# A transformer layer on one core: the seven products of w_o in another order, added up in PSUM banks

## The chip, the cores and the metric

The kernel runs on 1 core of a Trainium2 chip. A core has five engines with an instruction queue each: TensorE (PE, with PEld for its weight loads), VectorE (DVE), ScalarE (ACT), GpSimd (POOL) and SyncE (SP); 16 DMA engines move data between DRAM and the core's own memories, SBUF (128 partitions) and PSUM (here eight banks of 128 x 512 float32, into which TensorE writes). The metric is the time of one execution in microseconds; given is the median of three runs.

## The reference

One layer on x of 512 tokens by 2048 channels, in float32:

```python
h = rms_norm(x, pre_mix_g);  z = h @ w_in            # q, k, v (1024 each) and u (1024)
a = chunked_attention(q, k, v, rel_bias)              # 8 heads of 128
p = multiscale_pool(u, pool_w, pool_scale)            # windows 2, 4, 8, 16: mean of the window
                                                      # minus the token, times pool_w per group
m = concat([a, p]) @ w_o                              # (512 x 2048) @ (2048 x 2048)
x = x + rms_norm(m, post_mix_g)
h = rms_norm(x, pre_ffn_g)
up = causal_dwconv(h @ w_up)                          # 2 x 5632 columns
y = (gelu(up[:, :5632]) * up[:, 5632:]) @ w_down
x = x + rms_norm(y, post_ffn_g)
```

The change lies in the line of m and in the two below it.

## The kernel before, in words

**Products.** A float32 operand is split into a rounded part (hi, fp32r) and the rest (lo): `split` (L138) has ACT round (L140, or L143 with a scale) and DVE subtract (L141, L144). `mm3` (L161) multiplies with three matmuls: hi by hi, hi by lo, lo by hi (L162, L164, L165).

**Weights.** `Weights` goes through a list of slices (`specs`) in the order of use. A slice of 128 x 1024 is loaded by SP (L152) into one of five raw buffers, at most two slices ahead of its split, and split into one of four pairs of buffers, four slices ahead of the matmuls. So the split of a slice waits for its data and for TensorE's end with the slice four before it.

**w_o.** The mixing matrix `mixT` (attention and pooled channels, transposed) times w_o is cut into 2 x 2 blocks: tokens 0 to 255 and 256 to 511, input halves, output halves of 1024 columns. Instead of eight block products there are seven (numbers 1 to 7) of sums and differences of blocks. The left factors (a11, s3, a12, n1, s2, s4, a22) are made by DVE from `mixT` and split; the sums of w_o's blocks for products 5, 6, 7 and 4 were added up in DRAM earlier. `wo_product(i, cc, ...)` makes one product for one half cc of 512 columns: four weight slices of 24 matmuls into two banks. After a slice of every product but the first it takes one step of `ready_blocks`, which readies six parts of w_down's first blocks: an SP load (`rw`, L843), four steps later the split, then two stores, after which the buffer takes the next load.

The order before is 1, 7, 2, 5, 6, 3, 4. Each product gets new banks. ACT copies products 1, 7 and 5 out (`copy_out`), DVE adds the others to rows in SBUF (`add_out`); three adds of 128 x 2048 (L946, L948, L949) join the rows: `y12 += y16`, `y16 += y7`, `y7 += y12`. A block of rows is then squared and summed by ACT (`square`, L910), multiplied by the gain by DVE (`scaled`, L915), normed (`norm`, L963 to L968, one step on POOL) and added to the residual x (`x2`, L980). `turn_back` transposes it (L995, TensorE) for the next stage, and `split` scales the result into `gT`.

**The pooled channels.** The last window's differences come from `pool_keep(3, 1, u7)`: sums by DVE (L732) into `tmp` (L737 to L740), split into dh and dl. `pool_mix(3)` multiplies the two differences (0 and 1) with `pool_w` (slice pm3): twelve matmuls in two banks, which ACT writes into the last part of `mixT` (L756).

**The first gate products.** `gate_part` multiplies the first slices of w_up with `gT` of tokens 0 to 255; between the parts the transposes of tokens 256 to 511 and their gate parts follow.

**Order.** TensorE runs in the order in which the code is written. The other engines' order is made by the framework's scheduler when the program is built, and is fixed then; each engine runs its list from the top and stands still while the first instruction waits.

```python
ps1 = [wo_product(1, cc, a11) for cc in range(2)]
...
pool_mix(3, keep_mix)
```

Of the kernel before, what the change touches and what calls it, by code (L numbers as in the profile page):

```python
# [15 lines left out]
P = 128  # L16
# [65 lines left out]
def encoder_layer(ctx: ExitStack, tc: tile.TileContext, x, xT, vecs, rel, post_mix, post_ffn,  # L82
# [160 lines left out]
    WO = 1, 7, 2, 5, 6, 3, 4  # L243
    wo_sum = {i: [dram.tile([P, 8, 512], F32, name=f"wt{i}{cc}") for cc in range(2)] for i in (7, 5, 6, 4)}
# [28 lines left out]
    for i in WO:  # L273
        for cc in range(2):
            specs += wo_specs(i, cc)
        if i == 1:
            specs += pm_spec(3)
# [12 lines left out]
    def sums_in_dram():  # L290
# [27 lines left out]
        for step, i, at in ((copy, 7, (1, 1)), (add, 7, (0, 1)), (copy, 5, (0, 0)), (add, 5, (0, 1)),  # L318
                            (copy, 6, 5), (add, 6, (1, 1)), (copy, 4, 6), (add, 4, (1, 0))):
            yield from wo_step(step, i, at)  # L320
# [292 lines left out]
    with tc.tile_pool(name="p1", bufs=2, reuse_waits="tile") as p1:  # L613
# [241 lines left out]

        def wo_product(i, cc, left, between=None):
            ps = [bank(f"m{i}{cc}{t}") for t in range(2)]
            if cc and i in (2, 5, 6, 3):
                more_sums(1)
            for q in range(4):  # L860
                w = weights.get(f"wo{i}_{cc}_{q}")
                for j in range(2):
                    kb = 2 * q + j
                    for t in range(2):
                        mm3(ps[t], tuple(v[:, kb, t * P:(t + 1) * P] for v in left), part(w, j), kb == 0, kb == 7)
# [8 lines left out]
        ps1 = [wo_product(1, cc, a11) for cc in range(2)]  # L874

        for v, w in zip(half(0, 0), half(0, 1)):
            nc.vector.tensor_sub(v, v, w)
        s3 = wo_left("s3", 0, 0)
        pool_mix(3, keep_mix)

    x2d = [dram.tile([P, D], F32, name=f"x2d{t}") for t in range(2, NT)]

    with tc.tile_pool(name="p2", bufs=1, reuse_waits="tile") as p2:
# [4 lines left out]
        y16, y7 = rows2("y16"), rows2("y7")  # L888
# [15 lines left out]
        def add_out(y, cc, ps, other=None):  # L904
            for t in range(2):
                nc.vector.tensor_add(y[:, t, columns(cc)], ps[t], (other or y)[:, t, columns(cc)])
# [10 lines left out]
        for cc in range(2):  # L917
            copy_out(y16, cc, ps1[cc])
        a12 = wo_left("a12", 1, 0)
        for cc in range(2):  # L920
            copy_out(y7, cc, wo_product(7, cc, s3))

# [3 lines left out]
        y11 = rows2("y11")  # L926
        for cc in range(2):
            add_out(y11, cc, wo_product(2, cc, a12), y16)

        for v, w in zip(half(0, 0), half(1, 1)):  # L930
# [5 lines left out]
        y12 = rows2("y12")  # L936
        for cc in range(2):
            copy_out(y12, cc, wo_product(5, cc, n1))
# [4 lines left out]
        for cc in range(2):  # L943
            add_out(y16, cc, wo_product(6, cc, s2))

        nc.vector.tensor_add(y12, y12, y16)  # L946
        a22 = wo_left("a22", 1, 1, [acc8(f"a22{p}", "A", F32R).rearrange("p (a b) -> p a b", a=8) for p in "hl"])
        nc.vector.tensor_add(y16, y16, y7)  # L948
        nc.vector.tensor_add(y7, y7, y12)  # L949
        y21, y22 = y16, y7  # L950
        for t in range(2):
# [796 lines left out]
```

## Time and profile before

| what | us |
|---|---|
| median of 3 runs | 1858.12 |
| lowest and highest | 1855.53, 1862.51 |
| span of the profiled execution | 1857.4 |
| TensorE busy in it | 1843.6 |
| VectorE busy | 1540.8 |
| ScalarE busy | 1082.3 |
| products of w_o in it (first to last matmul) | 389.8 to 550.1 |
| first gate matmul | 551.9 |

The profile is of one execution, and its span is that execution's own time. A row of the timeline shows the start, the length, the engine, the line, the operation with its tiles (output, arrow, inputs), and in brackets how long the engine had stood idle and what released it. Buffer numbers are left out of names, so `wo_1r` is the second slice of four of some product, as loaded, `wo_1h` and `wo_1l` its two parts, and `m` a bank of a product. Matmuls are pipelined: the time between two starts is what one costs. The numbers in a row of a table by window are the stretch, its length, busy times of PE, PEld, DVE, ACT and POOL (with counts), the granted clock, and the DMA engines' share and GB/s.

### The profile page before, as it was taken

How to read it: one execution, taken by the hardware profiler on the slowest of the kernel's cores; microseconds unless marked ns; L12 is line 12 of the kernel's file. 1: busy time of each engine (PE TensorE's matmuls, PEld its weight loads, DVE VectorE, ACT ScalarE, POOL GpSimd, SP SyncE). 2: the span in 40 equal slices, each digit the busy share in tenths (PEclk: the TensorE clock that was granted, in tenths of full speed). 3: DMA queues.
4: the chain of work that ended last, by engine and by line, in shares of the span. 5: the costliest groups of instructions: out<-in, count | busy, mean ns of one | idle time of the engine just before them, and what ended most of it. 6: DMA issues, size and time to landing. Idle time of an engine off the chain costs nothing.

```text
span 1857.4 us, 25457 instructions
## 1 busy us (share of the span) xinstructions
PE 1843.6 (99%) x9598; PEld 1584.8 (85%) x9598; DVE 1540.8 (83%) x1804; ACT 1082.3 (58%) x1376; POOL 303.2 (16%) x402
## 2 busy tenths in 40 slices
PE   9999999999999999999999999999999999999998
PEld 7888888888878888888888888888888888888886
DVE  6988777887698988888888888888887899899876
ACT  7654455456464666566666665656655655565553
POOL 3411000100000122212222122121121001111101
PEclk9999999999999999999999999999999999999999
DMA  8599978999994798988888888899888967777785
GB/s 319 174 318 297 320 232 236 267 255 331 348 328 144 186 213 195 208 210 195 203 198 206 209 199 198 204 206 202 200 176 293 363 220 175 193 210 178 176 229 159
DMA packets 139338, 426.01 MB, mean 229 GB/s; under 512 B 11920, under 2 KB 15376, under 8 KB 133520
## 3 DMA queue, kind: packets, MB, share of 16 engines
q0 software_dynamic: 54864, 173.56, 46.1%
q1 hardware_dynamic: 84352, 250.84, 38.4%
q8 instruction: 75, 1.23, 0.3%
q14 instruction: 47, 0.39, 0.1%
HBM read 370.35 MB, written 104.33 MB: 256 GB/s over the span
## 4 chain that ended last, share of the span: by engine, by line
PE 93%; DMA 3%; DVE 2%; ACT 1%; issue 1%; SPq 0%; DVEq 0%; POOL 0%; POOLq 0%; ACTq 0%
PE qa L170 18%; PE qa L176 10%; PE qg L170 9%; PE qg L176 5%; PE qd L170 4%; PE pa L164 4%; PE pa L165 4%; PE pa L162 4%; PE qd L176 2%; PE pg L164 2%; PE pg L165 2%; PE pg L162 2%; PE m L164 2%; PE m L165 2%; PE m L162 2%; PE v L164 2%
## 5 line engine op out<-in xcount | busy, mean ns | idle before, releaser
L140 ACT ACTIVATE wfh<-wx 128x1024 fp32r<-128x1024 f32 x192 | 203.4, 1059 | 152.7 <-PE qg L170 55.4
L170 PE MATMUL qa<-gT,wfh 128*128 128x512 f32 x1152 | 288.6, 392 | 0.0
L141 DVE TENSOR_TENSOR wfl<-wx,wfh 128x1024 fp32r<-128x1024 f32 x192 | 234.7, 1222 | 59.8 <-ACT wfh L140 44.8
L170 PEld LDWEIGHTS qa<-gT,wfh 128*128 128x128 f32 x1152 | 207.2, 189 | 37.1
L1365 POOL DMA_DIRECT2D wx<-in_w_up x122 | 104.7, 858 | 502.2 <-DVE wfl L141 473.8
L140 ACT ACTIVATE wfh<-wy 128x1024 fp32r<-128x1024 f32 x96 | 101.7, 1060 | 109.3 <-PE qg L170 57.9
L170 PE MATMUL qg<-h,wfh 128*128 128x512 f32 x656 | 162.2, 389 | 0.9 <-ACT zb L1421 0.9
L176 PE MATMUL qa<-gT,wfl 128*128 128x256 f32 x1152 | 161.2, 283 | 0.1
L176 PEld LDWEIGHTS qa<-gT,wfl 128*128 128x128 f32 x1152 | 151.6, 191 | 4.3 <-ACT zm L1425 0.3
L170 PEld LDWEIGHTS qg<-h,wfh 128*128 128x128 f32 x656 | 122.9, 188 | 26.7 <-ACT zb L1421 1.3
L141 DVE TENSOR_TENSOR bl<-b,bh 128x2048 fp32r<-128x2048 f32 x56 | 127.2, 2287 | 19.1 <-ACT bh L140 11.7
L140 ACT ACTIVATE bh<-b 128x2048 fp32r<-128x2048 f32 x56 | 106.1, 1913 | 55.1 <-DVE b L1129 22.8
L141 DVE TENSOR_TENSOR wfl<-wy,wfh 128x1024 fp32r<-128x1024 f32 x96 | 117.2, 1221 | 10.9 <-ACT wfh L140 6.4
L162 PE MATMUL pa<-bh,ah 128*128 128x512 f32 x320 | 124.5, 389 | 0.0
L164 PE MATMUL pa<-bl,ah 128*128 128x512 f32 x320 | 124.5, 389 | 0.0
L165 PE MATMUL pa<-bh,al 128*128 128x512 f32 x320 | 124.5, 389 | 0.0
L141 DVE TENSOR_TENSOR wfl<-wz,wfh 128x1024 fp32r<-128x1024 f32 x48 | 58.7, 1224 | 54.1 <-PE qa L170 54.1
L176 PEld LDWEIGHTS qg<-h,wfl 128*128 128x128 f32 x656 | 89.5, 190 | 6.4
L170 PE MATMUL qd<-gT,wfh 128*128 128x512 f32 x384 | 94.9, 389 | 0.0
L176 PE MATMUL qg<-h,wfl 128*128 128x256 f32 x656 | 91.5, 282 | 0.0
L170 PEld LDWEIGHTS qd<-gT,wfh 128*128 128x128 f32 x384 | 72.0, 188 | 14.9
L170 PE MATMUL qa<-h,wfh 128*128 128x512 f32 x328 | 82.1, 392 | 0.0
(550 smaller groups left out, 4363.5 us busy)
## 6 DMA issues: line engine op xcount, KB each, us to landing
wx<-in_w_up POOLq DMA_DIRECT2D x122, 512.0 KB, 6.1
b<-in_w_down SPq DMA_DIRECT2D x32, 1024.0 KB, 6.8
wt<-in_w_o POOLq DMA_DIRECT2D x24, 1024.0 KB, 15.8
wx<-in_w_up SPq DMA_DIRECT2D x43, 512.0 KB, 5.5
wz<-in_w_up SPq DMA_DIRECT2D x41, 512.0 KB, 6.0
wy<-in_w_up SPq DMA_DIRECT2D x41, 512.0 KB, 4.6
wy<-in_w_up POOLq DMA_DIRECT2D x41, 512.0 KB, 6.9
sum<-part POOLq DMA_DIRECT2D x38, 512.0 KB, 6.8
```

What stands on the lines that cost most here:

```text
L140: rounded = nc.scalar.activation(hi, src, AF.Copy)
L141: rest = nc.vector.tensor_sub(lo, src, f32(hi))
L162: nc.tensor.matmul(ps, l[0], r[0], start=first, stop=False, skip_group_check=onto)
L164: nc.tensor.matmul(low, l[0], r[1], start=False, stop=False, skip_group_check=onto)
L165: nc.tensor.matmul(ps, l[1], r[0], start=False, stop=last, skip_group_check=onto)
L170: nc.tensor.matmul(ps, w[0][:, kb], pairs[kb][0], start=fresh and not kb, stop=last, skip_group_check=not fresh)
L176: nc.tensor.matmul(ps[:, sl], w[1][:, kb], pair[:, sl], start=False, stop=last, skip_group_check=not fresh)
L1365: nc.gpsimd.dma_start(self.raw[k, what], self.block(k, m, kh), accum_op=ALU.add)
```

## The change

The order becomes 1, 2, 5, 6, 3, 7, 4. Eight banks are named once: m0 to m3 serve products 1, 6, 7 and 4, m4 to m7 products 2, 5 and 3. Products 6, 3, 7 and 4 do not begin their banks anew but add onto what lies there (`ONTO`), so the rows come out as y11 = 1 + 2, y12 = (1 + 6) + (5 + 3), y22 = 5 + (1 + 6 + 7) and y21 = 1 + 6 + 7 + 4. The three wide adds go, and so do four of the adds from banks; y21 is squared and multiplied by the gain straight from the banks (`finish_last`). Tokens 0 to 255 (y11, y12) are complete with product 3, the fifth. Their transposes, eight groups of four, stood two behind each slice of product 4's second half; now one stands behind each slice of product 7's second half and of product 4's first, in banks m4 to m7. `pool_mix(3)` and its weight slice move from behind product 1 to between its two halves; a12 is split right behind product 1, and s3, now made as -s2 - a22, behind product 6.

The scheduler moves other engines with it. On SP, the loads around product 1's second half (`wo1_1_0r` is its first slice, `pm3r` the pooled weights, `pooled` and `mixT3` the pooled values that go through DRAM), before:

```order
L152 DMA wo1_0_3r_3834<-in_w_o 128x2x512
L152 DMA wo1_1_0r_3864<-in_w_o 128x2x512
L763 DMA pooled_360<-mx_3795 128x1024
L152 DMA wo1_1_1r_3928<-in_w_o 128x2x512
L823 DMA mixT3_3895<-pooled_360 128x1024
L152 DMA wo1_1_2r_3934<-in_w_o 128x2x512
L152 DMA wo1_1_3r_3952<-in_w_o 128x2x512
L152 DMA pm3r_3970<-in_pool_w 128x2x256
```

and after the change:

```order
L152 DMA wo1_0_3r_3834<-in_w_o 128x2x512
L152 DMA pm3r_3864<-in_pool_w 128x2x256
L763 DMA pooled_360<-mx_3795 128x1024
L152 DMA wo1_1_0r_3934<-in_w_o 128x2x512
L823 DMA mixT3_3895<-pooled_360 128x1024
L152 DMA wo1_1_1r_3940<-in_w_o 128x2x512
L152 DMA wo1_1_2r_3958<-in_w_o 128x2x512
L152 DMA wo1_1_3r_3976<-in_w_o 128x2x512
```

The pooled weights take the place of slice (1,0), and slice (1,1) now stands behind the reload of `mixT3`. On ACT the same place, where `dh1` is the rounding of the last pooled difference, before:

```order
L140 ACTIVATE wo1_1_0h_3936<-wo1_1_0r_3864 128x1024
L140 ACTIVATE wo1_1_1h_3954<-wo1_1_1r_3928 128x1024
L140 ACTIVATE wo1_1_2h_3972<-wo1_1_2r_3934 128x1024
L140 ACTIVATE dh1_3922<-tmp_3919 128x512
L140 ACTIVATE wo1_1_3h_3990<-wo1_1_3r_3952 128x1024
L140 ACTIVATE pm3h_4010<-pm3r_3970 128x512
```

and after:

```order
L140 ACTIVATE pm3h_3942<-pm3r_3864 128x512
L140 ACTIVATE wo1_1_0h_3960<-wo1_1_0r_3934 128x1024
L140 ACTIVATE wo1_1_1h_3978<-wo1_1_1r_3940 128x1024
L140 ACTIVATE dh1_3930<-tmp_3927 128x512
L140 ACTIVATE wo1_1_2h_3996<-wo1_1_2r_3958 128x1024
L756 ACTIVATE mixT3_3895<-pm3_0_4018,vec_69 128x512
```

`dh1` stood behind slice (1,2) and stands behind (1,1); the use of the pooled product (L756) follows two rows later. On DVE, the splits of product 3's slices (`wo3_0_2l` is the rest of slice 2 of its first half), before:

```order
L906 TENSOR_TENSOR y16_4115<-m611_4721,y16_4115 128x512
L946 TENSOR_TENSOR y12_4472<-y12_4472,y16_4115 128x2048
L141 TENSOR_TENSOR wo3_0_3l_4783<-wo3_0_3r_4744,wo3_0_3h_4782 128x1024
L948 TENSOR_TENSOR y16_4115<-y16_4115,y7_4116 128x2048
L141 TENSOR_TENSOR wo3_1_0l_4819<-wo3_1_0r_4762,wo3_1_0h_4818 128x1024
L949 TENSOR_TENSOR y7_4116<-y7_4116,y12_4472 128x2048
L141 TENSOR_TENSOR wo3_1_1l_4839<-wo3_1_1r_4780,wo3_1_1h_4838 128x1024
```

and after:

```order
L141 TENSOR_TENSOR wo3_0_3l_4609<-wo3_0_3r_4567,wo3_0_3h_4608 128x1024
L141 TENSOR_TENSOR wo3_1_0l_4642<-wo3_1_0r_4588,wo3_1_0h_4641 128x1024
L141 TENSOR_TENSOR wo3_1_1l_4660<-wo3_1_1r_4606,wo3_1_1h_4659 128x1024
L141 TENSOR_TENSOR rw_4741<-rw_4741,rwh_4742 128x1024
L141 TENSOR_TENSOR wo3_1_2l_4680<-wo3_1_2r_4639,wo3_1_2h_4679 128x1024
```

The wide adds between the splits are gone, and a part of w_down's blocks (`rw`) is split there. The diff:

```diff
--- before.py
+++ after.py
@@ -240,8 +240,8 @@
 
 
 
-    WO = 1, 7, 2, 5, 6, 3, 4
-    wo_sum = {i: [dram.tile([P, 8, 512], F32, name=f"wt{i}{cc}") for cc in range(2)] for i in (7, 5, 6, 4)}
+    WO = 1, 2, 5, 6, 3, 7, 4
+    wo_sum = {i: [dram.tile([P, 8, 512], F32, name=f"wt{i}{cc}") for cc in range(2)] for i in (5, 6, 7, 4)}
 
     def wo_block(cc, j, l):
         cs = slice(l * D // 2 + cc * 512, l * D // 2 + (cc + 1) * 512)
@@ -273,8 +273,8 @@
     for i in WO:
         for cc in range(2):
             specs += wo_specs(i, cc)
-        if i == 1:
-            specs += pm_spec(3)
+            if (i, cc) == (1, 0):
+                specs += pm_spec(3)
     for n in range(PLAIN):
         for u, p in (divmod(n, 2),):
             specs += [(f"w{p}{u}_{i}", w_up[u, p, :, i // 2, :, i % 2 * 512:(i % 2 + 1) * 512].rearrange(
@@ -315,8 +315,8 @@
                     step(wo_sum[i][cc][:, sl, :], source[:, sl, :])
                     yield
 
-        for step, i, at in ((copy, 7, (1, 1)), (add, 7, (0, 1)), (copy, 5, (0, 0)), (add, 5, (0, 1)),
-                            (copy, 6, 5), (add, 6, (1, 1)), (copy, 4, 6), (add, 4, (1, 0))):
+        for step, i, at in ((copy, 5, (0, 0)), (add, 5, (0, 1)), (copy, 6, 5), (add, 6, (1, 1)),
+                            (copy, 7, (1, 1)), (add, 7, (0, 1)), (copy, 4, 6), (add, 4, (1, 0))):
             yield from wo_step(step, i, at)
         for step, i, at in ((copy, 5, (0, 0)), (add, 5, (0, 1)), (copy, 7, (1, 1)), (copy, 6, 5),
                             (add, 7, (0, 1)), (add, 6, (1, 1)), (copy, 4, 6), (add, 4, (1, 0))):
@@ -853,8 +853,12 @@
 
         ready_steps = ready_blocks()
 
+        wo_banks = [bank(f"m{n}") for n in range(8)]
+        ONTO = 6, 3, 7, 4
+
         def wo_product(i, cc, left, between=None):
-            ps = [bank(f"m{i}{cc}{t}") for t in range(2)]
+            at = 2 * cc + (4 if i in (2, 5, 3) else 0)
+            ps = wo_banks[at:at + 2]
             if cc and i in (2, 5, 6, 3):
                 more_sums(1)
             for q in range(4):
@@ -862,7 +866,8 @@
                 for j in range(2):
                     kb = 2 * q + j
                     for t in range(2):
-                        mm3(ps[t], tuple(v[:, kb, t * P:(t + 1) * P] for v in left), part(w, j), kb == 0, kb == 7)
+                        mm3(ps[t], tuple(v[:, kb, t * P:(t + 1) * P] for v in left), part(w, j),
+                            i not in ONTO and kb == 0, kb == 7, i in ONTO)
                 if i != 1:
                     next(ready_steps, None)
                 if between:
@@ -871,12 +876,10 @@
 
         a11 = wo_left("a11", 0, 0)
         pool_keep(3, 1, u7)
-        ps1 = [wo_product(1, cc, a11) for cc in range(2)]
-
-        for v, w in zip(half(0, 0), half(0, 1)):
-            nc.vector.tensor_sub(v, v, w)
-        s3 = wo_left("s3", 0, 0)
+        ps1 = [wo_product(1, 0, a11)]
         pool_mix(3, keep_mix)
+        ps1.append(wo_product(1, 1, a11))
+        a12 = wo_left("a12", 1, 0)
 
     x2d = [dram.tile([P, D], F32, name=f"x2d{t}") for t in range(2, NT)]
 
@@ -885,7 +888,7 @@
 
             return p2.tile([P, 2, D // 2], F32, tag=name, name=name)
 
-        y16, y7 = rows2("y16"), rows2("y7")
+        y11, y12, y21, y22 = (rows2(f"y{n}") for n in (11, 12, 21, 22))
         gain = p2.tile([P, D], F32, name="gain")
         nc.sync.dma_start(gain, post_mix[None, :].to_broadcast([P, D]))
         small = p2.tile([P, 64], F32, name="small")
@@ -901,9 +904,9 @@
             for t in range(2):
                 nc.scalar.activation(y[:, t, columns(cc)], ps[t], AF.Copy)
 
-        def add_out(y, cc, ps, other=None):
+        def add_out(y, cc, ps):
             for t in range(2):
-                nc.vector.tensor_add(y[:, t, columns(cc)], ps[t], (other or y)[:, t, columns(cc)])
+                nc.vector.tensor_add(y[:, t, columns(cc)], ps[t], y[:, t, columns(cc)])
 
         def square(v, total):
             junk = p2.tile([P, D // 2], F32, tag="junk", name="junk")
@@ -915,43 +918,30 @@
             nc.vector.tensor_mul(y[:, :, cs], y[:, :, cs], g[:, None, :].to_broadcast([P, 2, cs.stop - cs.start]))
 
         for cc in range(2):
-            copy_out(y16, cc, ps1[cc])
-        a12 = wo_left("a12", 1, 0)
-        for cc in range(2):
-            copy_out(y7, cc, wo_product(7, cc, s3))
-
+            copy_out(y11, cc, ps1[cc])
         for v, w in zip(half(0, 1), half(1, 1)):
             nc.vector.tensor_sub(v, w, v)
         n1 = wo_left("n1", 0, 1)
-        y11 = rows2("y11")
         for cc in range(2):
-            add_out(y11, cc, wo_product(2, cc, a12), y16)
-
-        for v, w in zip(half(0, 0), half(1, 1)):
+            add_out(y11, cc, wo_product(2, cc, a12))
+        for v, w in zip(half(0, 0), half(0, 1)):
             nc.vector.scalar_tensor_tensor(v, v, -1.0, w, op0=ALU.mult, op1=ALU.subtract)
         s2 = wo_left("s2", 0, 0)
         for t in range(2):
             square(y11[:, t, :], ssq[:, t, 0:1])
         scaled(y11, 0)
-        y12 = rows2("y12")
         for cc in range(2):
-            copy_out(y12, cc, wo_product(5, cc, n1))
+            copy_out(y22, cc, wo_product(5, cc, n1))
 
         for v, w in zip(half(1, 0), half(0, 0)):
             nc.vector.scalar_tensor_tensor(v, v, -1.0, w, op0=ALU.mult, op1=ALU.subtract)
         s4 = wo_left("s4", 1, 0)
         for cc in range(2):
-            add_out(y16, cc, wo_product(6, cc, s2))
-
-        nc.vector.tensor_add(y12, y12, y16)
+            copy_out(y12, cc, wo_product(6, cc, s2))
+        for v, w in zip(half(0, 0), half(1, 1)):
+            nc.vector.scalar_tensor_tensor(v, v, -1.0, w, op0=ALU.mult, op1=ALU.subtract)
+        s3 = wo_left("s3", 0, 0)
         a22 = wo_left("a22", 1, 1, [acc8(f"a22{p}", "A", F32R).rearrange("p (a b) -> p a b", a=8) for p in "hl"])
-        nc.vector.tensor_add(y16, y16, y7)
-        nc.vector.tensor_add(y7, y7, y12)
-        y21, y22 = y16, y7
-        for t in range(2):
-            square(y22[:, t, :], ssq[:, 2 + t, 0:1])
-        scaled(y22, 1)
-
 
         def finish(y, cc, ps, t0, l, at):
 
@@ -986,9 +976,8 @@
                         square(xn[t][:, l * D // 2:(l + 1) * D // 2], ssq2[:, t, l:l + 1])
                 nc.sync.dma_start(x2d[t - 2] if t >= 2 else out[t * P:(t + 1) * P, :], xn[t])
 
-        def turn_back(t0, pair):
-
-            ps = bank(f"xt{t0}_{pair}")
+        def turn_back(t0, pair, ps):
+
             for k in range(2):
                 kb = 2 * pair + k
                 for t in range(2):
@@ -1005,20 +994,30 @@
         for t in range(2):
             load_x(t, acc8(f"x{t}", "B"))
         hT = new_gT()
-        ps4 = wo_product(4, 0, a22)
         x2(0, y11, 0, whole)
         x2(0, y12, 1, whole)
-        finish(y21, 0, ps4, 2, 0, 1)
-
-        def first_half(q):
-            for i in range(2):
-                turn_back(0, 2 * q + i)
-
-        ps4 = wo_product(4, 1, a22, first_half)
+
+        def first_half(at):
+            return lambda q: turn_back(0, at + q, wo_banks[4 + q])
+
+        for cc in range(2):
+            add_out(y22, cc, wo_product(7, cc, s3, first_half(0) if cc else None))
+        for t in range(2):
+            square(y22[:, t, :], ssq[:, 2 + t, 0:1])
+        scaled(y22, 1)
+
+        def finish_last(cc, ps):
+            g = gain[:, columns(cc)]
+            for t in range(2):
+                square(ps[t], ssq[:, 2 + t, 1 + cc:2 + cc])
+                nc.vector.tensor_mul(y21[:, t, columns(cc)], ps[t], g)
+
+        finish_last(0, wo_product(4, 0, a22, first_half(4)))
+        ps4 = wo_product(4, 1, a22)
         keep_x(0)
         for t in range(2):
             load_x(2 + t, p2.tile([P, D], F32, tag=("y11", "y12")[t], name=f"x{2 + t}"))
-        finish(y21, 1, ps4, 2, 0, 2)
+        finish_last(1, ps4)
         norm(2)
 
 
@@ -1041,7 +1040,7 @@
             if q < 4:
                 x2(2, (y21, y22)[q // 2], q // 2, columns(q % 2))
                 for i in range(2):
-                    turn_back(2, 2 * q + i)
+                    turn_back(2, 2 * q + i, bank(f"xt{q}{i}"))
             if not q:
                 gate_part(3, 0, slice(2, 4))
             if q:
```

## The prediction

> **What bounds the kernel now.** The page comes first: its span, its busy times and its chain.
>
> ```profile
> span 1857.4 us, 25457 instructions
> PE 1843.6 (99%) x9598; PEld 1584.8 (85%) x9598; DVE 1540.8 (83%) x1804; ACT 1082.3 (58%) x1376; POOL 303.2 (16%) x402
> PE 93%; DMA 3%; DVE 2%; ACT 1%; issue 1%; SPq 0%; DVEq 0%; POOL 0%; POOLq 0%; ACTq 0%
> ```
>
> TensorE is busy 99% of the span and makes 93% of the chain. The change keeps every matmul and every transpose, so only TensorE's idle stretches can move. I therefore read its waits from 380 to 600 us, where w_o's products and the first gate products lie:
>
> ```profile
> PE up L162 <- DVE gT L144: 1.6, 1, 1.6
> PE up L164 <- DVE gT L144: 0.7, 2, 0.5
> PE m L164 <- DVE wo_1l L141: 0.3, 1, 0.3
> ```
>
> The columns are the sum, the count and the longest; every wait is for VectorE. Matmul records overlap, so the true loss is read from starts. The weight wait is in product 3, on TensorE and then on VectorE:
>
> ```profile
> 509.61 0.39 PE L162 MATMUL m<-wo_3h,s 128*128 128x512 f32 x1
> 510.07 0.50 PE L164 MATMUL m<-wo_3l,s 128*128 128x512 f32 x1
> 510.41 0.40 PE L165 MATMUL m<-wo_3h,s 128*128 128x512 f32 x1
> ...
> 512.74 0.39 PE L162 MATMUL m<-wo_0h,s 128*128 128x512 f32 x1
> 513.41 0.50 PE L164 MATMUL m<-wo_0l,s 128*128 128x512 f32 x1 [0.28 <-DVE wo_0l L141]
> ...
> 516.04 0.39 PE L162 MATMUL m<-wo_1h,s 128*128 128x512 f32 x1
> 516.75 0.50 PE L164 MATMUL m<-wo_1l,s 128*128 128x512 f32 x1 [0.32 <-DVE wo_1l L141]
> ```
>
> ```profile
> 506.59 2.29 DVE L946 TENSOR_TENSOR y<-y,y 128x2048 f32<-128x2048 f32 x1
> ...
> 509.93 2.28 DVE L948 TENSOR_TENSOR y<-y,y 128x2048 f32<-128x2048 f32 x1
> 512.14 1.22 DVE L141 TENSOR_TENSOR wo_0l<-wo_0r,wo_0h 128x1024 fp32r<-128x1024 f32 x1
> 513.27 2.28 DVE L949 TENSOR_TENSOR y<-y,y 128x2048 f32<-128x2048 f32 x1
> ```
>
> A 512-wide matmul starts 0.23 us after the one before it. Against that, 509.61 to 510.07 loses 0.23, 512.74 to 513.41 loses 0.44 and 516.04 to 516.75 loses 0.48. The matmul behind a stalled one starts another 0.11 late (510.07 to 510.41), three times. Together 1.5 us. Each late weight half stands on VectorE right behind one of the three wide sums.
>
> The other two places are at the first gate products:
>
> ```profile
> 549.30 1.04 PE L995 MATMUL xt<-ident,x 128*128 128x128 f32 x8
> 551.94 0.36 PE L162 MATMUL up<-gT,w_0h 128*128 128x256 f32 x1 [1.60 <-DVE gT L144]
> ...
> 562.12 1.03 PE L995 MATMUL xt<-ident,x 128*128 128x128 f32 x8
> ...
> 565.21 0.36 PE L162 MATMUL up<-gT,w_0h 128*128 128x256 f32 x1
> 565.77 0.39 PE L164 MATMUL up<-gT,w_0h 128*128 128x256 f32 x1 [0.19 <-DVE gT L144]
> ...
> 566.47 0.28 PE L162 MATMUL up<-gT,w_0h 128*128 128x256 f32 x1
> 567.21 0.39 PE L164 MATMUL up<-gT,w_0h 128*128 128x256 f32 x1 [0.47 <-DVE gT L144]
> ```
> ```profile
> 560.60 4.72 DVE L980 SCALAR_TENSOR_TENSOR x<-y,small,x 128x512 f32<-128x512 f32 x7
> ```
>
> Eight transposes start 0.11 us apart, so without a wait the gate would begin near 550.2. It begins at 551.94, with a slow second start: 1.9 us lost to splitting transposes that all lie in product 4's second half. At 565.77 and 567.21, two starts of 0.12 us became 0.56 and 0.74, and each successor is 0.10 late: 1.3 us, behind the 4.72 us of residual sums of tokens 256 to 511.
>
> **The change, part by part.** (1) *The three wide sums and four of VectorE's adds go.* 6.85 us leave VectorE between the weight splits of product 3; the sums are now made by accumulating matmuls that exist already. Gain 1.5 us.
>
> (2) *Tokens 0 to 255 come out with the fifth product.* Their transposes and splits lie in product 7's second half and product 4's first, so the splits have the 10.9 us of product 4's second half (48 pairs of a 0.23 us step) as cover. Gain 1.9 us. Without that cover it comes back whole.
>
> (3) *Product 4 is squared and scaled straight from its banks.* A square of one bank stands so in the trace:
>
> ```profile
> 556.12 0.63 ACT L910 ACTIVATE junk<-y 128x512 f32<-128x512 f32 x1
> 556.65 0.19 ACT L910 ACTIVATION_READ_ACCUMULATOR junk<-y 128x1 f32 x1
> ```
>
> After the last matmul of product 4 I count one weight rounding on ScalarE (1.06, as any of its size), two squares with their read-outs (0.82 each), the norm's small steps before the first residual sum (1.25) and eight residual sums (5.4, at 4.72 for seven): 9.4 us. The gate matmuls before the next transposes take 551.94 to 562.12, less the 0.1 of the slow start 10.1. So the sums end 0.7 us ahead of the transposes, and no split stands behind them. Gain 1.3; it is the thinnest cover here, and its lower bound is 0.
>
> (4) *Transposes are spread, four behind each slice instead of eight.* Same number, more returns to matmuls:
>
> ```profile
> 539.22 0.48 PE L162 MATMUL m<-wo_1h,a22h 128*128 128x512 f32 x1
> 539.53 0.40 PE L164 MATMUL m<-wo_1l,a22h 128*128 128x512 f32 x1
> ```
>
> 539.22 to 539.53 is 0.31 instead of 0.23, which happens three times in product 4 now and eight times after: five more, cost 0.4 us.
>
> (5) *pool_mix(3) goes between product 1's two halves.* Its load takes the place in SP's queue of product 1's weight slice (1,0); that slice moves to the place of (1,1), which moves behind the reload of the pooled values, to the place where (1,2) stood. In ACT's order the last pooled difference dh stands behind the rounding of (1,1), and in VectorE's order dl stands behind that slice's subtraction. What the place costs in the present trace, on SP, ACT and VectorE, then the flight times and TensorE:
>
> ```profile
> 391.82 1.12 SPq L152 DMA_DIRECT2D wo_2r<-in_w_o  x1
> ```
> ```profile
> 402.39 1.06 ACT L140 ACTIVATE wo_2h<-wo_2r 128x1024 fp32r<-128x1024 f32 x1 [4.68 <-DMA wo_2r<-in_w_o]
> 403.35 0.62 ACT L140 ACTIVATE dh<-tmp 128x512 fp32r<-128x512 f32 x1
> ```
> ```profile
> 401.30 0.17 DVE L739 TENSOR_TENSOR tmp<-uf,u 128x16 f32<-128x16 f32 x1
> ...
> 404.62 0.69 DVE L141 TENSOR_TENSOR dl<-tmp,dh 128x512 fp32r<-128x512 f32 x1
> ```
> ```profile
> wo_1r<-in_w_o SPq DMA_DIRECT2D x1, 512.0 KB, 15.0
> wo_2r<-in_w_o SPq DMA_DIRECT2D x1, 512.0 KB, 10.5
> ```
> ```profile
> 400.71 0.39 PE L162 MATMUL m<-wo_0h,a 128*128 128x512 f32 x1
> ```
>
> Now nobody feels it: the pooled product runs at 411.6, long after dl. In the change it begins where product 1's second half begins, 400.71. Its first three matmuls use the first difference; the fifth needs dl, 4 steps of 0.23 later, at 401.62. If the slice lands as wo_2r does now (391.82 + 10.5 = 402.3), ACT rounds it at 402.39, dh follows at 403.35, dl ends at 405.31: 3.7 us late. Ahead of it 256 KB less is in flight; at 436 GB/s (the window row further down, a full one) that makes it at most 0.6 earlier: 3.1 us late. I take the middle, 3.4, and 0.1 for the slow successor: cost 3.5 us. Below, had the slice landed long before, the pool chain alone decides: tmp at 401.47, dh 0.62, dl 0.69 give 402.85, so 1.3 us late, 1.4 in all. Above, with the 15.0 us flight of the slice before, it lands at 406.8 and the cost is 8.3.
>
> (6) *The parts of w_down's first block* are still readied one after another, but fall on other slices. ACT stands still for them now:
>
> ```profile
> 500.77 1.06 ACT L140 ACTIVATE rwh<-rw 128x1024 fp32r<-128x1024 f32 x1 [5.22 <-DMA rw<-in_w_down]
> ```
>
> Even 5.22 us left TensorE nothing to wait for by itself: the losses begin with the sums. A weight split is made up to four slices (10.9 us) ahead. I put 0.3 us, the largest wait for one weight half above; the bounds are 0 and 4, a further hold of nearly such a length once the lead is used up.
>
> The rest is covered: s3 and a12 are made products ahead of use, and each bank is copied or added out at least one product half (10.9 us) before the next product writes it.
>
> Sum: −1.5 −1.9 −1.3 +0.4 +3.5 +0.3 = −0.5 us, so a span of 1856.9. The median of the runs, 1858.12, stands 0.7 above the profiled span: 1857.6 us.
>
> A rule of the Trainium skill speaks against the change, and the sum without it stays: "TensorE: Matmul & The Clock Gate", Part 1, says that TensorE drops to half its clock after an idle window of about 3.4 us. What the trace has is shorter:
>
> ```profile
> 549.00:552.00 3.00, 1.40 (x12) 1.05 (x10) 2.36 (x5) 3.00 (x8) 0.00 (x0) 1.00 1.04 436
> ```
>
> Across the 1.60 us wait the granted clock (the 1.00) stayed full. The new wait has two pieces, about 2.5 us for dh and 1.0 for dl, with one matmul between.
>
> **The rivals.**
> *A, the new wait hardly shows.* The slice lands early and 1.4 us is left: 1857.6 − 2.1 = 1855.5. For it: VectorE's chain allows it. Against: no slice issued near 391 lands in under 10 us.
> *B, the other side: the slice lands late.* It decides from a landing near 402.8, 0.5 us after wo_2r's, where the new wait eats all 4.0 us of net gain. With 15.0 us of flight the cost is 8.3 and the time 1857.6 + 4.8 = 1862.4. For it: that flight time, one place earlier in the same queue. Against: the slice that has the place now took 10.5.
> *C, the readying of w_down holds ACT inside another product.* 4 instead of 0.3: 1861.3. For it: holds of 5.22 us exist. Against: VectorE now has 6.85 us less to do behind them.
> *D, the gains are passed on.* The gate waits for something else at 550, or the residual sums are late: −1.9 and −1.3 fall away, 1860.8. For it: the 0.7 us of cover in (3). Against: its weights are split products ahead.
> *E, TensorE is slow again after the new wait, as at the program's start.*
>
> ```profile
> 1.09 4.21 PE L133 MATMUL idle<-early 128*128 128x128 f32 x18 [1.09 <-DVE mhalf L129]
> ```
>
> 18 matmuls of this size take 4.21 us there, 0.21 apart instead of the transposes' 0.11. As long a stretch after the wait would lose about 2 us: 1859.6. For it: the new wait is longer than any here. Against: full speed after 1.60 us, and the wait has a matmul in its middle. This is what the Trainium skill's rule above would give if both pieces counted as one window.
>
> **How the numbers follow.** Forecast 0.50, A 0.15, B 0.12, C 0.10, D 0.08, E 0.05. The likeliest is 1857.6. No removed wait is worth more than 4.7 us together, so below 1853 little is left, with the runs of before lying 2.6 under and 4.4 above their median. Upwards the range takes in B to D: 1852.5 to 1863.5, with the likeliest's own range 1855 to 1860. A measurement of this kernel can tell about 0.5%, 9.3 us, from no change. All cases lie within that; faster by more 0.02, slower by more 0.04 (B and C together, or an engine that I misjudged), within 0.94.
>
> **What would show it.** Right: a wait of PE pm for dh and dl of 2.5 to 4 us near 401; none left for L946 to L949; the first gate matmul directly behind product 4; no wait for gT near 566. Wrong: pm starting without a wait (A), over 5 us there (B), m waiting for weight halves in products 5 to 7 (C), up waiting at its first matmuls (D), pairs of matmuls 0.4 us or more apart after 405 (E).

## The result and the profile after

The change makes the kernel slower by 0.4%: 1864.49 us, the median of 6 runs (1863.39 to 1868.34), against 1857.41 us for the kernel before (6 runs, 1855.16 to 1862.51). The ratio is 1.0042, 95% interval 1.0028 to 1.0056. Forecast were 1857.6 us and a range up to 1863.5.

The page of the changed kernel, its span, busy times and chain:

```profile
span 1861.6 us, 25449 instructions
PE 1844.7 (99%) x9598; PEld 1584.7 (85%) x9598; DVE 1532.4 (82%) x1799; ACT 1083.8 (58%) x1376; POOL 303.4 (16%) x402
PE 92%; DMA 5%; DVE 2%; ACT 1%; issue 1%; SPq 0%; DVEq 0%; POOLq 0%; ACTq 0%
```

Against the page of the kernel before, VectorE has 8.4 us less to do, and DMA has gone from 3% to 5% of the chain. TensorE's waits between 380 and 600 us (sum, count, longest):

```profile
PE m L162 <- ACT wo_3h L140: 2.0, 1, 2.0
PE m L164 <- DVE wo_3l L141: 1.6, 2, 1.0
PE pm L162 <- ACT dh L140: 1.3, 1, 1.3
PE pm L164 <- DVE dl L141: 0.8, 1, 0.8
```

The waits for `gT` at the first gate products and for the weights of product 3 are gone. In their place stand the pooled product (`pm`), as forecast, and one weight slice each in products 5 and 6 (a `wo_3` in both, so that `wo_3l` counts two). Product 6, on TensorE:

```profile
480.38 0.39 PE L165 MATMUL m<-wo_2h,s 128*128 128x512 f32 x1
482.81 0.49 PE L162 MATMUL m<-wo_3h,s 128*128 128x512 f32 x1 [2.04 <-ACT wo_3h L140]
484.26 0.50 PE L164 MATMUL m<-wo_3l,s 128*128 128x512 f32 x1 [0.95 <-DVE wo_3l L141]
...
486.01 0.63 PE L164 MATMUL m<-wo_3l,s 128*128 128x512 f32 x1
486.44 0.63 PE L165 MATMUL m<-wo_3h,s 128*128 128x512 f32 x1
486.87 0.63 PE L162 MATMUL m<-wo_3h,s 128*128 128x512 f32 x1
```

The two starts lose 2.20 and 1.22 us against a step of 0.23, the next another 0.11. Then the matmuls start 0.43 us apart for a while, without a wait. The windows over that place show it in the third number from the end, the granted clock: it is 1.00, then 0.50.

```profile
482.00:484.00 2.00, 0.49 (x1) 0.19 (x1) 2.00 (x2) 2.00 (x4) 0.00 (x0) 1.00 0.95 401
484.00:486.00 2.00, 1.74 (x6) 1.38 (x7) 1.50 (x3) 2.00 (x3) 0.00 (x0) 0.86 0.90 286
486.00:488.00 2.00, 2.00 (x6) 1.60 (x5) 2.00 (x2) 1.20 (x3) 0.00 (x0) 0.50 0.78 264
488.00:490.00 2.00, 2.00 (x8) 1.59 (x8) 1.15 (x2) 1.50 (x2) 0.00 (x0) 0.79 0.60 129
```

What TensorE waited for stood behind a part of w_down's blocks on ScalarE; ScalarE and SP at that place:

```profile
472.34 1.06 ACT L140 ACTIVATE wo_2h<-wo_2r 128x1024 fp32r<-128x1024 f32 x1 [1.66 <-DMA wo_2r<-wt]
480.76 1.06 ACT L140 ACTIVATE rwh<-rw 128x1024 fp32r<-128x1024 f32 x1 [7.36 <-DMA rw<-in_w_down]
481.72 1.04 ACT L140 ACTIVATE wo_3h<-wo_3r 128x1024 fp32r<-128x1024 f32 x1
```
```profile
466.25 0.42 SPq L850 DMA_DIRECT2D rw11l<-rw  x1
...
468.56 0.38 SPq L152 DMA_DIRECT2D wo_1r<-in_w_o  x1
476.14 0.37 SPq L843 DMA_DIRECT2D rw<-in_w_down  x1
```

The data for `wo_3h` had landed at 474.9. ScalarE stood 7.36 us at `rwh`, whose load SP could issue only at 476.14, when the store of the part before it (issued at 466.25) had landed.

From one profile to the other, by TensorE's starts: product 3 −1.6, first gate matmul −1.9, the `gT` waits −1.3; returns from transposes +0.5 (eight of 0.09 instead of three); pooled product +2.7 (1.46, 1.11, 0.11); product 5 +1.0; product 6 +3.5 of waiting and +1.6 of slow starts. Sum +4.5; the spans differ by 4.2. The median differs by 7.1 because the two profiled executions stand differently among their runs: in every execution with both on record a time is 1.7 to 1.9 us above its span, so the profile of before (1857.4) belongs to an execution of some 1859.2 (an estimate; none of the six has that time), 1.8 over their median, and the one of the change (1863.39) is the fastest of its six.

### The profile page after: what moved, and what is told of

It reads as the page before. It is cut to its first block, busy times and chain, and to the rows that moved or that the text cites. A ratio compares the mean times of both kernels' runs of the same rounds, so it can differ in the third digit from the quotient of the medians.

```text
span 1861.6 us, 25449 instructions
## 1 busy us (share of the span) xinstructions
PE 1844.7 (99%) x9598; PEld 1584.7 (85%) x9598; DVE 1532.4 (82%) x1799; ACT 1083.8 (58%) x1376; POOL 303.4 (16%) x402
## 4 chain that ended last, share of the span: by engine, by line
PE 92%; DMA 5%; DVE 2%; ACT 1%; issue 1%; SPq 0%; DVEq 0%; POOLq 0%; ACTq 0%
PE qa L170 18%; PE qa L176 10%; PE qg L170 9%; PE qg L176 5%; PE qd L170 4%; PE pa L162 4%; PE pa L164 4%; PE pa L165 4%; PE qd L176 2%; PE m L164 2%; PE m L165 2%; PE m L162 2%; PE pg L162 2%; PE pg L164 2%; PE pg L165 2%; PE v L165 2%
## 5 line engine op out<-in xcount | busy, mean ns | idle before, releaser
L141 DVE TENSOR_TENSOR bl<-b,bh 128x2048 fp32r<-128x2048 f32 x56 | 127.2, 2286 | 19.0 <-ACT bh L140 11.7
```

The source lines that it names most:

```text
L141: rest = nc.vector.tensor_sub(lo, src, f32(hi))
```

## The experiments

Each ratio is to the kernel before, measured beside it. Losses in a profile are read from TensorE's starts.

**The pooled product back behind product 1** (specs and call as in the kernel before, all else of the change kept):

```diff
-        ps1 = [wo_product(1, 0, a11)]
+        ps1 = [wo_product(1, cc, a11) for cc in range(2)]
         pool_mix(3, keep_mix)
-        ps1.append(wo_product(1, 1, a11))
```

> The change, but pool_mix(3) and its weight slice stand again behind the whole of product 1. With that alone the scheduler also puts the roundings of w_down's parts (rwh) five to seven slices later in ScalarE's order, the first behind slice (0,0) of product 5 and not behind (0,3) of product 2. Theory (the loss is the wait of the pooled product at 403 us, 2.7 us, and the two holds of rwh in products 5 and 6 with the slow stretch behind them, 6.1 us): all of it goes, TensorE's waits in the seven products come to under 1 us, and the time is 2 to 4 us under the kernel before, ratio 0.998 to 0.999. Rival (the new product order or adding up in PSUM costs by itself): only 2.7 us come back, ratio about 1.0025.

Measured: ratio 1.0001 (0.9990 to 1.0013), 1858.95 us. The expectation was wrong on the order: the parts come only two or three slices later than in the change (the first behind slice (1,1) of product 2). No wait of `pm` is left, and no slow start in the products. ScalarE still stands at `rwh`, 5.32 us at 470.22, and TensorE waits 2.1 us in product 6:

```profile
PE m L164 <- DVE wo_0l L141: 1.0, 1, 1.0
PE m L162 <- ACT wo_0h L140: 0.6, 1, 0.6
```

So taking back that one move takes back nearly all of the loss, some 7.6 us by the ratios for a wait of 2.7, since the parts move with it. By the time alone the new order of products neither gains nor loses. In the profile, the stretch from product 1's first matmul to the first gate matmul is 0.7 us shorter than before (161.4 against 162.1), with the wait of 2.1 us still in it. Product 1 begins 2.7 us later than before (392.57 against 389.83) in this execution, with a stretch of half clock at 12.45 in the products for q and k, which the edit leaves alone. So the wait that stayed is one reason that the kernel did not get faster than before, as the theory said, and the spread between executions another.

**The parts of w_down's blocks later on ScalarE**, the pooled product left between the halves:

```diff
-                split(hi, lo, v)
+                with tc.issue_after(split.last):
+                    split(hi, lo, v)
```

> The change, with one order constraint: ScalarE rounds each part of w_down's blocks only behind the weight split that the program has made by then, so the parts stand five to seven slices later. The pooled product stays between product 1's halves. Theory: its wait of 2.7 us stays, the 6.1 us of products 5 and 6 go, ratio 0.9995 to 1.001. Rival (the parts' loads are late wherever they stand, so the hold only moves to another product): ratio 1.003 to 1.005, with a wait of the same size behind an rwh elsewhere.

Measured: 1.0009 (0.9998 to 1.0021), 1860.66 us. No idle time stands before any of the six `rwh`; the waits in products 5 and 6 and the slow starts are gone, the pooled product waits 2.9 us (2.7 in the change). The rival falls: a later place in the queue is enough. One wait of 1.7 us came up in product 7, where four residual sums on VectorE stand ahead of a weight split:

```profile
513.10 4.87 DVE L971 SCALAR_TENSOR_TENSOR x<-y,small,x 128x1024 f32<-128x1024 f32 x4
517.88 1.22 DVE L141 TENSOR_TENSOR rw<-rw,rwh 128x1024 fp32r<-128x1024 f32 x1
519.02 1.22 DVE L141 TENSOR_TENSOR wo_1l<-wo_1r,wo_1h 128x1024 fp32r<-128x1024 f32 x1
```

**The wait in product 6 filled with matmuls of zeros.**

```diff
                 w = weights.get(f"wo{i}_{cc}_{q}")
+                if (i, cc, q) == (6, 1, 3):
+                    for _ in range(20):
+                        nc.tensor.matmul(ps[0][:, :P], early, early, start=False, stop=False, skip_group_check=True)
```

> The change, with 20 matmuls of 128x128 of zeros added onto a bank of product 6 just ahead of its last slice, where TensorE waits 2.2 us (they add nothing, and take about 2.2 us at full speed). Theory (the seven to eight matmuls that start 0.43 us apart behind that wait do so because TensorE had been idle): they start 0.23 us apart again, the wait itself stays, and the time falls by about 1.7 us, ratio 1.002 to 1.004 with the change at 1.0042. Rival (the slow starts come from what runs beside them): the slow starts stay and the time is that of the change or up to 2 us more, ratio 1.004 to 1.006.

Measured: 1.0070 (1.0049 to 1.0092), 1871.56 us; as a time neither theory's. The 20 are recorded as 40 and took 4.4 us, and the scheduler moved the later parts forward. But the place itself answers: behind the fill the matmuls keep their 0.23 us, at full clock.

```profile
481.50 4.63 PE L868 MATMUL m<-early 128*128 128x128 f32 x40
485.88 0.48 PE L162 MATMUL m<-wo_3h,s 128*128 128x512 f32 x1
486.20 0.39 PE L164 MATMUL m<-wo_3l,s 128*128 128x512 f32 x1
486.43 0.39 PE L165 MATMUL m<-wo_3h,s 128*128 128x512 f32 x1
```

A part now held ScalarE for 9.93 us in product 3; TensorE lost 2.14 and 1.22 us there, and a dozen matmuls behind it started 0.43 us apart at a granted clock of 0.50. The slow starts went with the idleness.

**The kernel before with the pooled product alone moved** between product 1's halves, by the same edit the other way round:

> The kernel before with one part of the change: pool_mix(3) and its weight slice between the halves of product 1. Theory (this one move makes the pooled product wait, and draws the parts of w_down forward): a wait of 2.5 to 4 us for dh and dl near 403, and rwh one to six slices earlier with new waits in the middle products; ratio 1.0015 to 1.005. Rival (the loss needs the new product order): the pooled product's wait alone or none, ratio 1.000 to 1.0015.

Measured: 1.0057 (1.0038 to 1.0076), 1869.65 us, at the upper end of the theory's range or above. The pooled product loses 2.4 and 1.1 us at 406 and 407, and here the slow stretch follows at once, 12 starts 0.43 us apart, 2.9 us with the steps into and out of it:

```profile
404.00:406.00 2.00, 0.00 (x0) 0.00 (x0) 0.51 (x1) 1.59 (x3) 0.00 (x0) 1.00 1.05 423
406.00:408.00 2.00, 1.12 (x3) 0.71 (x4) 2.00 (x3) 0.93 (x1) 0.00 (x0) 0.63 0.58 226
408.00:410.00 2.00, 2.00 (x6) 1.61 (x5) 2.00 (x4) 0.69 (x1) 0.00 (x0) 0.50 0.97 242
```

In product 3, where the kernel before loses 1.6 us, 4.0 are lost. That makes 8.9 of the 11.3 us between the two spans; most of the rest (2.2) is lost ahead of product 1, around 346, where the profile names VectorE's `us` (the pooled sums) and the rounding `qkh` as what TensorE waits for; the run doesn't say whether the move causes it. The rival falls: the loss doesn't need the new order.

**Both corrections**: the pooled product back and the parts later.

> The change with both: pool_mix(3) behind the whole of product 1, and the parts of w_down's blocks (rwh) held to their place in the program, as in the run with rwh later. Theory (the two waits are separate and add): against that run the 2.9 us of the pooled product go, no wait behind an rwh comes in their place, and of TensorE's waits only the one in product 7 (1.7 us, behind four residual sums on VectorE) and the returns from transposes (0.7) are left; ratio 0.9985 to 0.9995. Rival (the chain of load, split and store paces the products, so that TensorE, coming 2.9 us earlier, waits for it elsewhere, as it did for 2.0 us at 472 in the run with the pooled product back): ratio 1.000 to 1.001.

Measured: 0.9991 (0.9982 to 1.0001), 1856.85 us. One wait is left in the products, the 1.8 us behind the residual sums. Against the run with the parts later, 1.0009 to 0.9991 is 3.3 us for a wait of 2.9 (2.8 by the starts of the two profiles), as two separate causes would have it; the two intervals just overlap. Against the change the two corrections don't add: alone they bring 0.0041 and 0.0033, together 0.0051, which fits that putting the pooled product back also moves the parts later.

**The residual sums apart**, on top of that:

```diff
         x2(0, y11, 0, whole)
-        x2(0, y12, 1, whole)
...
-        for cc in range(2):
-            add_out(y22, cc, wo_product(7, cc, s3, first_half(0) if cc else None))
+        add_out(y22, 0, wo_product(7, 0, s3))
+        with tc.issue_after(split.last):
+            x2(0, y12, 1, whole)
+        add_out(y22, 1, wo_product(7, 1, s3, first_half(0)))
```

> The same, and of the four residual sums of tokens 0 to 255 two (those of y12) are made behind product 7's first half instead of all four in a row. Theory: the wait for a weight half in product 7 (1.7 us) goes too, the transposes of product 4's first half find their columns ready, and under 1 us of waits is left in the products: ratio 0.997 to 0.9985, below the kernel before. Rival (the sums that move make something else late in product 4): ratio as the run without it or above.

Measured: 0.9988 (0.9977 to 0.9998), 1856.84 us. The wait in product 7 is gone, but 1.5 us came up near 473 in product 6, where a weight slice lands late; the gain over the run with both corrections alone is not resolved, and the time lies between the two forecasts.

**The pooled difference ahead of the late slice** on ScalarE and VectorE, in the change as it is:

```diff
         pool_keep(3, 1, u7)
+        first_of["wo1_1_1"] = split.last, split.rest
...
```

(`round_w`, in lines not shown, splits a slice only behind what `first_of` names for it.)

> The change, with one order constraint: the split of product 1's slice (1,1) comes behind the split of the last pooled difference on ScalarE and VectorE. The parts of w_down's blocks come one slice later with it. Theory (the pooled product waits because its difference stands behind a slice that is still in flight, not for the difference itself): the wait near 403 falls from 2.7 us to under 0.5, the holds in products 5 and 6 stay or shrink; ratio 1.001 to 1.003. Rival (the difference itself is late): the wait stays above 1.5 us and the ratio at 1.004.

Measured: 1.0013 (1.0005 to 1.0022), 1861.84 us. The pooled product still loses 0.39 and 0.85 us and a slow successor, 1.35 in all, half of the 2.7: the other half was the place in the queue. That is about what the prediction gave the chain of the difference alone (1.4). Some 6 us of waits stay in products 5, 3 and 7, single or in pairs of 0.7 to 1.2 us, without a slow stretch. The pooled wait lies between the bounds of both theories; the queue and the difference itself share it.

**A ladder of idle stretches** behind the kernel before's last store.

```diff
+        for first, second in LADDER:
+            nc.scalar.activation(src[:, :8], ps[:, :8], AF.Copy)
+            if second:
+                chain(va, first)
+                chain(vb, second)
+                nc.tensor.matmul(one, va[:, :P], va[:, :512], start=True, stop=True)
+            else:
+                chain(vb, first)
+            burst(50, vb)
```

The first copy waits for the burst before; `chain` makes so many copies of 128x1024, `burst` so many matmuls of 128x512.

> The kernel before, with an appendix behind its last store: bursts of 50 matmuls of 128x512 of zeros with idle stretches of growing length ahead of them (ScalarE copies of about 0.95 us each hold them back: 1, 2, 3, 4, 5 of them, three times over; then pairs of stretches with a single matmul between, 1+1, 2+1, 1+2, 2+2, three times). Its time as a whole means nothing. Theory (slow starts come from idleness gathered over some 3.4 us): none after stretches of 1.5 and 2.5 us, always after 4.5 and more, and the pairs behave nearly as one stretch of their sum. Rival (only the length of the single wait counts): the pairs 1+1, 2+1 and 1+2 show none.

Measured, by the starts of the bursts (the step is 0.23 us at full speed; "slow" are starts 0.35 to 0.6 us apart):

| start to start before the burst, us | slow starts, three tries |
|---|---|
| 1.80 | 0, 0, 0 |
| 2.89 | 7, 0, 0 |
| 3.98 | 8, 8, 8 |
| 5.07 | 14, 14, 14 |
| 6.15 | 7, 6, 6 |
| 1.80, one matmul, 0.95 | 8, 8, 8 |
| 1.80, one matmul, 2.04 | 0, 7, 8 |
| 3.69, one matmul, 0.95 | 6, 7, 7 |
| 3.97, 3.69, 3.69 (the pair 2+1; ScalarE made all three copies ahead of the single matmul) | 8, 0, 0 |

Two of the stretches on TensorE, one of them the shortest pair, and windows behind them:

```profile
1957.13 1.65 PE L1714 MATMUL burst<-vb 128*128 128x512 f32 x6 [1.41 <-ACT vb L1718]
...
2121.00 0.50 PE L1726 MATMUL one<-va 128*128 128x512 f32 x1 [1.42 <-ACT va L1718]
2121.95 4.46 PE L1714 MATMUL burst<-vb 128*128 128x512 f32 x12 [0.45 <-ACT vb L1718]
```
```profile
1905.00:1909.00 4.00, 4.00 (x12) 3.11 (x11) 0.00 (x0) 0.00 (x0) 0.00 (x0) 0.61 0.00 0
2122.00:2126.00 4.00, 4.00 (x12) 3.22 (x13) 0.00 (x0) 0.00 (x0) 0.00 (x0) 0.65 0.00 0
```

Slow starts follow every single stretch of 3.97 and more, none of 1.80, one of three of 2.89 and neither of two of 3.69; in between it is not the same each time. A single matmul in the middle does not save it, so the rival falls: the pair of 1.80 and 0.95 was slow each time, each time some matmuls after its end.

What decides in between is on record in the granted clock. In all twelve profiles, once it is full (4 to 7 us after the start), it changes only at the edges of a grid of 3.41 us. In the products and in the ladder every stretch at 0.50 lasts one or two windows of that grid, 3.41 or 6.83 us. Count as idle what lies between two starts beyond 0.23 us (an estimate). Then each of the 26 stretches of half clock ahead of a program's end follows a window with 2.07 us or more of idleness, and none of the some 6500 windows that are followed by full clock has more than 2.08. So the idleness within one window decides, whether in one piece or two, and not a sum of 3.4 us as the theory had it; a stretch is slow or not by where it falls on the grid. The three tries are therefore not independent: the half clocks behind 3.98 us begin at 1904.72, 1986.64 and 2068.56, 24 windows apart each time, so each try meets nearly the same place of the grid.

The Trainium skill, "TensorE: Matmul & The Clock Gate", Part 1, has half clock after an idle window of about 3.4 us, and lets the windows run on from before the stretch. The length of the windows and their running on agree with the grid above; but no window has to be idle throughout: the single stretch of 2.89 and the pair of 1.80 and 0.95, both followed by half clock, hold no idle window of that length.

**The change once more**, for a second profile:

> The change once more, on one chip with the run below and with a second profile. Theory (its loss is the pooled product's wait, the holds behind rwh in products 5 and 6 and slow stretches whose length differs from run to run): the same two places wait in the new profile, to within 0.5 us each, and the runs spread over 4 us or more with a median 6 to 8 us over the kernel before; ratio 1.003 to 1.005. Rival (the first profile caught something that comes and goes): other places wait.

Measured: 1.0049 (1.0036 to 1.0062), 1867.82 us, with five runs from 1866.86 to 1869.91, closer together than expected, and 8.4 us over the kernel before where 6 to 8 were forecast. The same places wait, but not to within 0.5 us: the pooled product by 1.1 us longer and product 6 by 1.3, and now both are followed by a slow stretch:

```profile
PE m L162 <- ACT wo_3h L140: 3.4, 1, 3.4
PE pm L162 <- ACT dh L140: 2.4, 1, 2.4
PE m L164 <- DVE wo_3l L141: 1.9, 2, 0.9
PE pm L164 <- DVE dl L141: 0.8, 1, 0.8
```

Behind the pooled product 12 starts are slow (2.9 us with the steps into and out of it), which the first profile, waiting 1.46 + 1.11 instead of 2.60 + 1.11 us, did not have. The wait is longer because TensorE came to it 0.9 us earlier (third matmul at 400.20 instead of 401.09) and the slice ahead of `dh` landed 0.2 later: it was issued at 392.81 instead of 391.38 and flew 8.5 us instead of 9.7. The grid says why only this one is slow. In the first profile the wait lies across an edge, and the window that holds most of it has 1.97 us of idleness; in the second one window has 2.92. The two windows and what follows each, in the first and the second profile:

```profile
400.10:403.51 3.41, 1.87 (x8) 0.98 (x6) 1.27 (x2) 2.36 (x3) 0.00 (x0) 1.00 1.05 407
403.51:406.92 3.41, 2.80 (x12) 2.35 (x13) 2.85 (x4) 1.69 (x3) 0.00 (x0) 1.00 0.88 314
```
```profile
400.16:403.58 3.42, 0.92 (x3) 0.19 (x2) 1.79 (x4) 2.18 (x3) 0.00 (x0) 1.00 0.99 385
403.58:406.99 3.41, 2.62 (x6) 2.14 (x7) 3.03 (x5) 1.03 (x2) 0.00 (x0) 0.50 0.70 230
```

Runs near 1868 among the first six may be such executions; they were not profiled. Their mean granted clock points that way: 0.998 in the two runs near 1863.4, 0.997 in the other four, and 0.996 in four of the five here.

**The reload later**: the run with the sums apart, and the load of a part one slice later behind the stores.

```diff
-                for _ in range(4):
+                for _ in range(3):
                     yield
                 with tc.issue_after(split.last):
                     split(hi, lo, v)
...
-                for _ in range(2):
+                for _ in range(3):
                     yield
```

> The run with the residual sums apart, and the load of each part of w_down's blocks stands one slice later behind the stores of the part before (its split one slice earlier after it). Theory (SP stands still at that load until the stores have landed, and the weight loads behind it come late, which made the 1.5 us wait near 473): that wait falls under 0.5 us; ratio 0.9975 to 0.9985. Rival (the weight loads are late from traffic alone): the wait stays at 1 to 2 us, or a hold behind rwh comes back; ratio 0.9985 to 1.000.

Measured: 0.9981 (0.9972 to 0.9991), 1854.99 us. The wait near 473 shrinks from 1.5 to 0.4 us: the late slice's load, which stands behind the reload on SP in both, goes out at 457.24 instead of 459.83, though it flies 12.4 us instead of 11.7. That bears out the theory that SP stood at the reload. The reload itself stands ahead of the same slice as before; what moved is the store ahead of it, which goes out at 451.79 instead of 453.58 because the split comes a slice earlier. Of the losses in the products only 0.4 and the 0.7 of the transposes are left. This version is faster than the kernel before by 0.2%, and than the change.

## Why the prediction was wrong

*Steps 1 to 4 held.* Product 3 waits for nothing, the first gate matmul follows product 4 at once, no `gT` wait is left near 566.

```profile
557.44 0.39 PE L165 MATMUL m<-wo_3h,a22l 128*128 128x512 f32 x1
557.67 0.28 PE L162 MATMUL up<-gT,w_0h 128*128 128x256 f32 x1
```

The cover of step 3 is as thin as worked out: the residual sums end 0.5 us before the transposes that read them (0.7 forecast).

```profile
561.90 5.38 DVE L970 SCALAR_TENSOR_TENSOR x<-y,small,x 128x512 f32<-128x512 f32 x8
```
```profile
567.75 1.03 PE L984 MATMUL xt<-ident,x 128*128 128x128 f32 x8
```

The transposes cost 0.46 for 0.4. Rival D fell.

*Step 5 named the right wait* and gave 3.5 us for 2.7: the slice was issued 0.4 earlier and flew 9.7 us instead of 10.5. In the second profile the same wait is 3.7 long, plus the slow stretch. So the size was good, and two consequences were left out: the slow stretch, and that the same move brings the parts of step 6 forward. Giving ScalarE the difference first takes back half. (The parts of the lower bound add up to 402.78, not 402.85, which changes nothing.)

*Step 6 failed: "I put 0.3 us".* It took one hold of 5.22 us that hurt nobody as proof that such holds do not hurt. That hold had used up the whole lead of its slice: behind it, in the kernel before, ScalarE and VectorE make the two parts of slice (0,1) of product 3, and the second is ready at 504.22, while TensorE is there at 504.30.

```profile
501.73 1.05 ACT L140 ACTIVATE wo_1h<-wo_1r 128x1024 fp32r<-128x1024 f32 x1
```
```profile
503.00 1.22 DVE L141 TENSOR_TENSOR wo_1l<-wo_1r,wo_1h 128x1024 fp32r<-128x1024 f32 x1
```
```profile
504.30 0.47 PE L164 MATMUL m<-wo_1l,s 128*128 128x512 f32 x1
```

In the change ScalarE stands at five of the six parts, 29.8 us together (idle time ahead of `rwh`), where the five of before make 16.6. What one hold costs depends on its place: 6.84 us ahead of 521.13 cost nothing, 7.42 ahead of 444.43 cost 1.0 in product 5, and 7.36 ahead of 480.76 cost 3.5 in product 6. There the part stands ahead of slice (1,3), whose data had landed at 474.9, 5.7 us before TensorE was through with (1,2) at 480.6, and not the 10.9 of a full lead. (A slice is twelve matmuls of 0.23 us in these traces, not 24 as said ahead of the prediction; four slices are 10.9 us.) That earlier holds had eaten the rest of the lead fits the trace and is not shown by itself. The built order shows which slice each part stands ahead of; the prediction only said that the parts "fall on other slices". That is rival C, which had a chance of 0.10 and a price of 4 us; it measured 4.5. The run with only the parts later shows it: the waits in products 5 and 6 go, and the ratio is 1.0009.

*Rival E came on top*, at C's place and not at the new wait (1.6 us of slow starts), and in other executions at both. Its chance of 0.05 rested on "the wait has a matmul in its middle", which the ladder refutes. C and E were held apart as rivals; a wait of C's that leaves more than about 2.1 us of one window idle brings E with it.

*The base.* The prediction took the median as 0.7 above the profiled span, as if the two were of one execution. A time is about 1.8 above its own span, so the profiled execution was slower than the median, by 1.1 us for the three runs then known and 1.8 for the six. The waits were counted in one execution and taken off the time of another; against a loss of 7.1 us this is small.

What stays open: why TensorE reaches the products up to 3.7 us apart from one profile to another (388.9 to 392.6), and which stretches of half clock the unprofiled runs had.

## What to carry to other kernels

When a change moves work of a program whose other engines are ordered by a scheduler, count in the built order how many slices of lead each waiting instruction still leaves to the engine that sets the end; a hold that cost nothing is only proof for its own place. Price TensorE's idle time from some 2 us on with the slow stretch that may follow (1.6 us for one of 3.4, 2.9 for one of 6.8 here), and add up gaps with a few matmuls between. A load into the only buffer of a chain makes its queue stand still for the store before it, and the loads behind it come late: let the store go out early enough, as the last run did.

## What was not expected of the hardware

One matmul between two idle stretches of 1.80 and 0.95 us (start to start) did not keep the clock: all three tries ran 8 starts at 0.43 us. Some 2.07 us of idleness in a window of 3.41 us were enough. After a stretch of 5.07 us 14 starts were slow, after one of 6.15 only 6 or 7, so the slow stretch doesn't grow with the idle one: it was two windows of half clock (6.83 us) after the first and one (3.41) after the second. A float32 matmul of 128x128 of zeros was recorded as two, 0.11 us each.
